# First mixer: S5 input products in two PSUM pools, LRU tiles emitted in five steps

## The chip, the cores and the metric

One core of a Trainium2 chip runs the whole program. The metric is the device time in microseconds (us), the median of the runs. Five engines appear below: PE (TensorE matmuls; PEld is its weight loads), DVE (VectorE), ACT (ScalarE), POOL (GpSimd) and SP (SyncE, which issues the DMAs). Each works through its own queue in order and waits at an instruction until what that needs is done.

## The reference, cut to what matters

The program is a trunk of two layers on 1040 tokens of width 1024 (16 learned meta tokens are put in front of 1024). Each layer is a token mixer and an MLP with squared ReLU, each added to the residual. The change lies in the first mixer, which projects the normed input to 12 blocks of 128 features (four blocks x for the LRU, four blocks g for its gate, four blocks u for S5), and then:

```
x  = causal conv of width 4 over tokens (x)                    # per feature
r  = sigmoid(block_diag(x, w_a) + b_a);  i = sigmoid(block_diag(x, w_x) + b_x)
a  = exp(-8 * r * softplus(-lam));       m = sqrt(1 - a*a)
h[t] = a[t] * h[t-1] + m[t] * i[t] * x[t]                      # scan over tokens
y_lru = h * gelu(g)
# S5: 32 groups of 16 channels, 64 complex states each
s[t] = A * s[t-1] + B u[t];  y = real(C s) + d * u
y_s5 = gelu(y) * sigmoid(block_diag(gelu(y), w_glu) + b_glu)
out  = concat(y_lru, y_s5) @ w_out
```

## The kernel before

Features lie on the 128 partitions and tokens along the free dimension, cut in three stretches of 400, 384 and 256 (`TT`). A projection product is done as three float32r matmuls of split operands (`mm3`: high by high, high by low, low by high), so a *unit* (`unit`), one block of 128 output features for one stretch of tokens, is 8 x 3 = 24 matmuls into one PSUM bank, followed by a conversion on DVE (L969 for u, L978 for x, L984 and L986 for g). PSUM has eight banks here, in two pools of four: `mm` (`self.mm()`, used by units, the LRU gates, the S5 products and the S5 gate) and `sm` (`self.sm()`, used by the norm sums and the S5 tables).

`ev_units` gives 36 units in a fixed order, numbered 0 to 35 in the texts: u0 and u1 interleaved (0 to 5), u2 (6 to 8), u3 (9 to 11), x0 (12 to 14), x1 (15 to 17), g0 (18 to 20), x2 (21 to 23), x3 (24 to 26), g1 (27 to 29), and g2 and g3 mixed (30 to 35). The loop at the end of `mixer0` calls `events()` ahead of unit n and then emits the unit. Other work is hung onto these events by `at(n, (key, generator))`; the events of one n run in the order of their keys:

- S5 is computed in eight batches of four groups. `s5_tables` builds the matrices of a batch (L793 to L795 on DVE, transposes L806 and products L807 on PE, L813 on DVE, then L824 on PE and L826 on ACT). `s5_batch` loads the input of the batch, makes the input products (L848, L849) in two rounds, each with two PSUM tiles `va` and `vb`, multiplies them with rotations (L852, L853, L854), scans (L856), rotates back (L858 on POOL, L859) and makes the output products (L866 to L868). `s5_tile` takes two batches together: gelu (L884), gate matmul (L886), tanh (L887), and the product L888, which writes block 4 + t of the residual tile `h`.
- After the third unit of an x block, whose conversions are followed by the convolution (`lru_conv`: L900 on ACT, three L902 on DVE), `lru_tile` is run for that block: at n = 15, 18, 24 and 28 for blocks 0, 1, 2 and 3.

`lru_tile` has 48 instructions: six gate matmuls (L917) with sigmoids (L918), tanh, exp and a product (L920 to L922), a Newton step for the square root (L925 to L929), and per stretch a square root (L932), two products (L933 on DVE; L934 on POOL, for the last stretch on DVE) and the scan (L935). Its gate tiles `l_tr` and `l_ti` have one buffer each, so the sigmoids of one block wait until the scans of the block before are done. Its temporaries `th` and `q` are blocks 6 and 7 of `h`, which `s5_tile` writes for t = 2 and 3.

The order on each engine is not the program's: the framework's scheduler takes, for an engine that is free in its own model of time, the ready instruction of the highest priority. The priority is the place in the program, and `high_priority(offset=-100)` moves the instructions in it 100 places back (L60 to L63 set these offsets for the decorated functions; `lru_tile` has -100 in the first mixer). So a late place decides only among ready instructions. PSUM and SBUF tiles of a pool are given out in the order in which the scheduler comes to them.

Of the kernel before, what the change touches and what calls it, by code (L numbers as in the profile page):

```python
# [13 lines left out]
AF = mybir.ActivationFunctionType  # L14
ALU = mybir.AluOpType
# [7 lines left out]
TT = [(0, 400), (400, 384), (784, 256)]  # L23
# [55 lines left out]
class Trunk:  # L79
# [749 lines left out]
    def s5_batch(self, pool, b):  # L829

        nc, s5 = self.nc, self.s5
        v = nc.vector
        ud, yd = (q[b // 2][(b % 2) * 64:(b % 2) * 64 + 64] for q in (self.ud, self.yd))
        gs = slice(NG * b, NG * b + NG)
        ug = pool.tile([P, NG, 130], F32, name="s5ug", bufs=2)
        for g in range(NG):
            nc.sync.dma_start(ug[:, g], ud[16 * g:16 * g + 16].rearrange("c j n -> j c n"))
        yield
        M2, F, G, Z = self.tab[b]
        C, Sn = Z[:, 0], Z[:, 1]  # L840
        w = pool.tile([P, NG, 131], F32, name="s5w")
        w2 = pool.tile([P, NG, 131], F32, name="s5w2")
        v.memset(w[:, :, 0:1], 0.0)
        for g0 in range(0, NG, 2):
            n = 2
            va, vb = self.mm(), self.mm()
            for g in range(n):
                nc.tensor.matmul(va[:, g * 130:g * 130 + 130], lhsT=M2[:, g0 + g, 0:P], rhs=ug[:, g0 + g], start=True, stop=True)  # L848
                nc.tensor.matmul(vb[:, g * 130:g * 130 + 130], lhsT=M2[:, g0 + g, 64:192], rhs=ug[:, g0 + g], start=True, stop=True)  # L849
            v3 = lambda q: q[:, :n * 130].rearrange("p (g c) -> p g c", g=n)  # L850
            sl = (slice(None), slice(g0, g0 + n), slice(1, 131))
            v.tensor_tensor(out=w[sl], in0=v3(va), in1=C[sl], op=ALU.mult)  # L852
            v.tensor_tensor(out=w2[sl], in0=v3(vb), in1=Sn[sl], op=ALU.mult)  # L853
            v.tensor_tensor(out=w[sl], in0=w[sl], in1=w2[sl], op=ALU.add)  # L854
        for g in range(NG):
            v.tensor_tensor_scan(out=w[:, g, 1:], data0=s5["rho"][:, NG * b + g:NG * b + g + 1].broadcast_to([P, 130]), data1=w[:, g, 1:],  # L856
                                 initial=0.0, op0=ALU.mult, op1=ALU.add)
        nc.gpsimd.tensor_tensor(out=w2[:, :, 0:130], in0=w[:, :, 0:130], in1=Sn[:, :, 0:130], op=ALU.mult)  # L858
        v.tensor_tensor(out=w, in0=w, in1=C, op=ALU.mult)  # L859
        yield  # L860
        yg = pool.tile([P, NG, 130], F32, name="s5yg")
        m2 = lambda q: q.rearrange("p j i -> p (j i)")
        M1 = self.tab.pop(b)[4]
        for g in range(NG):
            pt = self.mm()
            nc.tensor.matmul(pt[:, :130], lhsT=m2(M1[:, g]), rhs=ug[:, g], start=True, stop=False)  # L866
            nc.tensor.matmul(pt[:, :130], lhsT=m2(F[:, g]), rhs=w[:, g, 0:130], start=False, stop=False)
            nc.tensor.matmul(pt[:, :130], lhsT=m2(G[:, g]), rhs=w2[:, g, 0:130], start=False, stop=True)  # L868
            nc.scalar.copy(yg[:, g], pt[:, :130])
        for g in range(NG):  # L870
            nc.sync.dma_start(yd[16 * g:16 * g + 16].rearrange("c j n -> j c n"), yg[:, g])
# [29 lines left out]
        for k in (2, 1, 0):  # L901
            nc.vector.scalar_tensor_tensor(out=xc, in0=xr[:, o + k:o + k + w], scalar=cw(k), in1=xc, op0=ALU.mult, op1=ALU.add)  # L902

    @shifted
    def lru_tile(self, pool, t):

        nc = self.nc
        v = nc.vector
        tr, ti = (pool.tile([P, NTOK], F32, name=n) for n in ("l_tr", "l_ti"))
        c = self.m0c  # L910
        m4, m8 = c["m4sp"][:, t:t + 1], c["m8sp"][:, t:t + 1]
        xc, th, q = ([self.h[i][:, k] for i in range(3)] for k in (t, 6, 7))
        trs, tis = ([d[:, o:o + w] for o, w in TT] for d in (tr, ti))
        for i, (o, w) in enumerate(TT):
            for j, d in enumerate((trs, tis)):
                pt = self.mm()
                nc.tensor.matmul(pt[:, :w], lhsT=c["gates"][:, j, t], rhs=xc[i], start=True, stop=True)  # L917
                nc.scalar.activation(out=d[i], in_=pt[:, :w], func=AF.Sigmoid, bias=self.col(("ba", "bx")[j], t))  # L918
        for i in range(3):
            nc.scalar.activation(out=th[i], in_=trs[i], func=AF.Tanh, scale=m4)  # L920
            nc.scalar.activation(out=q[i], in_=trs[i], func=AF.Exp, scale=m8)
            (nc.gpsimd if i < 2 else v).tensor_tensor(out=tis[i], in0=tis[i], in1=xc[i], op=ALU.mult)  # L922
        for i in range(3):
            m = trs[i]
            nc.scalar.activation(out=q[i], in_=q[i], func=AF.Copy, scale=0.5, bias=0.5)  # L925
            v.scalar_tensor_tensor(out=m, in0=th[i], scalar=-1.0, in1=q[i], op0=ALU.add, op1=ALU.mult)
            v.scalar_tensor_tensor(out=q[i], in0=m, scalar=2.0, in1=q[i], op0=ALU.add, op1=ALU.mult)
            v.tensor_tensor(out=m, in0=th[i], in1=q[i], op=ALU.mult)
            nc.scalar.activation(out=m, in_=m, func=AF.Identity, scale=2.0, bias=1.0)  # L929
        ini = 0.0  # L930
        for i, (o, w) in enumerate(TT):
            nc.scalar.activation(out=th[i], in_=th[i], func=AF.Sqrt, scale=-4.0)  # L932
            v.tensor_tensor(out=q[i], in0=q[i], in1=th[i], op=ALU.mult)  # L933
            (nc.gpsimd if i < 2 else v).tensor_tensor(out=tis[i], in0=tis[i], in1=q[i], op=ALU.mult)  # L934
            v.tensor_tensor_scan(out=xc[i], data0=trs[i], data1=tis[i], initial=ini, op0=ALU.mult, op1=ALU.add)  # L935
            ini = xc[i][:, w - 1:w]

    def unit(self, wt, i, tls, evac, more=0):

# [94 lines left out]
    def mixer0(self):  # L1034
        nc, tc, A = self.nc, self.tc, self.A
        with tc.tile_pool(name="m0c", reuse_waits="tile", bufs=1) as cpool, tc.tile_pool(name="m0", reuse_waits="tile", bufs=1) as m0:
# [46 lines left out]
            def at(n, g):  # L1083
                ev.setdefault(n, []).append(g)


            for b, s in enumerate((10, 13, 16, 19, 22, 25, 27, 30)):
# [7 lines left out]
                if b % 2:  # L1095
                    g = self.s5_tile(m0, b // 2)
                    for j in range(3, 7):
                        at(s + j, (1, g))
            n = 6
            lru = {}  # L1100
            gates, split = 0, 0

            def events():
                for _, g in sorted(ev.pop(n, []), key=lambda e: e[0]):
                    next(g, None)
                if n in lru:

                    assert self.s5_out < 2
                    self.lru_tile(m0, lru[n])

            while True:
                events()
                if gates == 1 and split == 0:
                    self.wo0 = self.load_w(A["ev_out"][0])
                while split < min(gates, self.s5_done):
                    self.split_y(split)
                    split += 1
                u = next(units, None)
                n += 1
                if u is None:  # L1120
                    if split == 3:
                        break
                    continue
                q, i = u
                if q[0] == "x":
                    self.lru_conv(int(q[1]), i, self.xr[int(q[1])])
                    if i == 2:
                        lru[n + (q == "x3")] = int(q[1])
                gates += q == "g3"
# [582 lines left out]
```

## Time and profile before

| | us |
|---|---|
| median of 3 runs (lowest, highest) | 2751.69 (2750.94, 2755.02) |
| the profiled execution, its own time | 2751.07 |
| its span in the trace | 2749.3 |
| busy: PE, DVE, ACT, POOL | 2664.6, 1963.5, 1076.9, 1034.7 |

Busy times are those of the whole span; an engine that waits at an instruction is idle. The granted clock of PE is given as a share of full speed (1.00 is 2.4 GHz, 0.50 is 1.2 GHz), averaged over the stretch asked for. Times in the trace count from the start of the span. The first mixer ends, and the output projection begins, at about 289 us.

### The profile page before, as it was taken

Reading aid. Unit: us, or ns where it says so; the run is one execution under the profiler, and the core shown is the slowest. Engines: PE = TensorE matmul, PEld = TensorE weight load, DVE = VectorE, ACT = ScalarE, POOL = GpSimd, SP = SyncE. Lnnn points to the kernel's source line nnn. Section 1 sums busy time; section 2 is a strip of 40 time slices with the busy share of each in tenths; the row PEclk is TensorE's granted clock in tenths of the full one; section 3 lists DMA queues with packets and bytes.
Section 4 is the critical chain, followed back from the end, with each engine's and each line's share of the span. In section 5 each row is a group of like instructions: output and inputs, shape, how many; then the busy total and the mean of one; then the engine's idle time right before and its main releaser. Section 6 shows DMA issues by size and latency. Waiting matters only on the chain.

```text
span 2749.3 us, 44507 instructions
## 1 busy us (share of the span) xinstructions
PE 2664.6 (97%) x17121; PEld 2551.6 (93%) x17121; DVE 1963.5 (71%) x3877; ACT 1076.9 (39%) x2207; POOL 1034.7 (38%) x842
## 2 busy tenths in 40 slices
PE   7998999999999999999999999999989999999998
PEld 7887999999999999899999999998988999999998
DVE  9887465666666686876767767677786666666685
ACT  5565344233233233453434434344454333333334
POOL 2122115454444532142233322333444554554542
PEclk9989999999999999999999999999999999999999
DMA  4422411111111110121211212123311111111111
GB/s 165 112 76 57 148 47 47 47 54 43 51 51 47 51 39 29 44 94 59 69 62 60 76 59 69 62 60 97 109 55 64 54 51 50 54 50 50 47 43 62
DMA packets 117909, 176.35 MB, mean 64 GB/s; under 512 B 13376, under 2 KB 47936, under 8 KB 117568
## 3 DMA queue, kind: packets, MB, share of 16 engines
q1 hardware_dynamic: 117408, 173.34, 20.3%
q8 instruction: 135, 2.21, 0.3%
q14 instruction: 78, 0.64, 0.1%
q10 hardware_dynamic: 288, 0.15, 0.0%
HBM read 158.34 MB, written 8.72 MB: 61 GB/s over the span
## 4 chain that ended last, share of the span: by engine, by line
PE 51%; DVE 6%; ACT 1%; DMA 1%; POOL 1%; issue 0%; DVEq 0%; ACTq 0%; POOLq 0%; SPq 0%
PE mm L182 12%; PE mm L183 12%; PE mm L184 12%; PE pd L182 3%; PE pd L184 3%; PE pd L183 3%; DVE xbc L1272 1%; PE mm L1392 1%; PE sm L1396 1%; PE mm L1389 1%; PE sm L1358 1%; DMA csb<-csd 1%; PE sm L253 1%; PE sm L270 0%; PE sm L1372 0%
## 5 line engine op out<-in xcount | busy, mean ns | idle before, releaser
L182 PE MATMUL mm<-hi,whi 128*128 128x384 f32 (+4 forms) x3120 | 1019.0, 327 | 16.1 <-ACT whi L176 8.6
L183 PE MATMUL mm<-lo,whi 128*128 128x384 f32 (+4 forms) x3120 | 1007.5, 323 | 0.9 <-DVE lo L300 0.5
L184 PE MATMUL mm<-hi,wlo 128*128 128x384 f32 (+4 forms) x3120 | 1004.2, 322 | 2.3 <-POOL wlo L177 2.3
L182 PEld LDWEIGHTS mm<-hi,whi 128*128 128x128 f32 x3120 | 591.0, 189 | 26.0 <-ACT whi L176 9.4
L183 PEld LDWEIGHTS mm<-lo,whi 128*128 128x128 f32 x3120 | 590.9, 189 | 7.2 <-DVE lo L300 0.8
L184 PEld LDWEIGHTS mm<-hi,wlo 128*128 128x128 f32 x3120 | 592.5, 190 | 3.3 <-POOL wlo L177 3.0
L182 PE MATMUL pd<-pc 128*128 128x260 f32 (+1 forms) x1176 | 377.0, 321 | 6.3 <-DVE s L375 2.2
L184 PE MATMUL pd<-pc 128*128 128x260 f32 (+1 forms) x1176 | 374.7, 319 | 0.0
L183 PE MATMUL pd<-pc 128*128 128x260 f32 (+1 forms) x1176 | 373.6, 318 | 0.0
L492 DVE TENSOR_TENSOR h<-h,pd 128x520 f32<-128x520 f32 (+1 forms) x336 | 291.8, 870 | 59.6 <-PE pd L184 45.2
L375 DVE SCALAR_TENSOR_TENSOR s<-mm,rb 128x384 f32<-128x384 f32 (+2 forms) x192 | 98.6, 514 | 265.1 <-PE mm L184 252.2
L389 POOL TENSOR_TENSOR pc<-ca,pc 128x512 fp32r<-128x512 f32 x112 | 169.8, 1516 | 244.8 <-ACT pc L388 164.1
L389 POOL TENSOR_TENSOR pc<-draw,pc 128x512 fp32r<-128x512 f32 x84 | 125.1, 1489 | 338.2 <-ACT pc L388 338.2
L182 PEld LDWEIGHTS pd<-pc 128*128 128x128 f32 x1176 | 221.5, 188 | 22.1 <-DVE acc L492 4.5
L184 PEld LDWEIGHTS pd<-pc 128*128 128x128 f32 x1176 | 221.6, 188 | 15.9
L183 PEld LDWEIGHTS pd<-pc 128*128 128x128 f32 x1176 | 221.6, 188 | 12.5
L176 ACT CAST whi<-wraw 128x512 fp32r<-128x512 f32 x286 | 167.6, 616 | 164.1 <-PE mm L183 150.2
L376 ACT ACTIVATE sq<-s 128x384 f32<-128x384 f32 (+2 forms) x192 | 94.1, 490 | 347.1 <-DVE s L375 347.0
L492 DVE TENSOR_TENSOR acc<-acc,pd 128x520 f32<-128x520 f32 (+1 forms) x234 | 190.3, 861 | 4.2 <-PE pd L184 4.1
L177 DVE TENSOR_TENSOR wlo<-wraw,whi 128x512 fp32r<-128x512 f32 x224 | 167.0, 764 | 18.1 <-ACT whi L176 9.4
L1378 POOL TENSOR_TENSOR csb<-csb,sc 128x512 f32<-128x512 f32 x64 | 89.7, 1402 | 210.3 <-DVE sc L1374 199.1
L388 ACT CAST pc<-cb 128x520 fp32r<-128x520 f32 (+1 forms) x112 | 70.0, 625 | 247.2 <-PE pd L184 130.4
(390 smaller groups left out, 4531.6 us busy)
## 6 DMA issues: line engine op xcount, KB each, us to landing
wraw<-in_mlp_up SPq DMA_DIRECT2D x128, 256.0 KB
wraw<-in_ssd_in SPq DMA_DIRECT2D x120, 256.0 KB
draw<-in_mlp_down SPq DMA_DIRECT2D x112, 256.0 KB
csb<-csd SPq DMA_DIRECT2D x64, 256.0 KB
ecb<-ecd SPq DMA_DIRECT2D x128, 64.0 KB
wraw<-in_ssd_out SPq DMA_DIRECT2D x32, 256.0 KB
wraw<-in_ev_in SPq DMA_DIRECT2D x24, 256.0 KB
wraw<-in_ev_out SPq DMA_DIRECT2D x18, 256.0 KB
```

Source lines behind the costliest of these rows:

```text
L176: nc.scalar.copy(h, raw)
L177: e.tensor_tensor(out=l, in0=raw, in1=h.bitcast(F32), op=ALU.subtract)
L182: nc.tensor.matmul(pt, lhsT=whi, rhs=xhi, start=first, stop=False)
L183: nc.tensor.matmul(pt, lhsT=whi, rhs=xlo, start=False, stop=False)
L184: nc.tensor.matmul(pt, lhsT=wlo, rhs=xhi, start=False, stop=last)
L253: nc.tensor.matmul(st[:l, 508 + i:509 + i], lhsT=a[:, o:o + l], rhs=self.ones, start=j == 0, stop=j == len(accs) - 1)
L375: nc.vector.scalar_tensor_tensor(out=r, in0=pt[:, :w], scalar=0.0, in1=rbs[i], op0=ALU.max, op1=ALU.mult)
L376: nc.scalar.activation(out=dst[:, o - t0:o - t0 + w].bitcast(F32), in_=r, func=AF.Square)
L388: nc.scalar.copy(hi, x)
L389: e.tensor_tensor(out=lo, in0=x, in1=hi.bitcast(F32), op=ALU.subtract)
L492: v.tensor_tensor(out=d, in0=d, in1=src, op=ALU.add)
L1378: nc.gpsimd.tensor_tensor(out=csb, in0=csb, in1=sc.unsqueeze(1).broadcast_to([P, 4, P]), op=ALU.mult)
```

## The change

Of the two tiles of an S5 round, `vb` is taken from the `sm` pool and no longer from `mm`. `lru_tile` loses its decorator and becomes a generator of five steps, each emitted 50 places back: gates and sigmoids; tanh, exp, products and the Newton step of stretch 0; the Newton steps of stretches 1 and 2 and all square roots; the products and scan of stretch 0; those of stretches 1 and 2. For blocks 0 to 2 the first two steps are emitted at the event where the whole tile was, and the others at the events of the next three units, with key 4; for block 3 all five are emitted at once. The arithmetic is the same. The order within a tile differs in that the square roots of all stretches come before the first product L933.

```diff
--- before.py
+++ after.py
@@ -843,7 +843,7 @@
         v.memset(w[:, :, 0:1], 0.0)
         for g0 in range(0, NG, 2):
             n = 2
-            va, vb = self.mm(), self.mm()
+            va, vb = self.mm(), self.sm()
             for g in range(n):
                 nc.tensor.matmul(va[:, g * 130:g * 130 + 130], lhsT=M2[:, g0 + g, 0:P], rhs=ug[:, g0 + g], start=True, stop=True)
                 nc.tensor.matmul(vb[:, g * 130:g * 130 + 130], lhsT=M2[:, g0 + g, 64:192], rhs=ug[:, g0 + g], start=True, stop=True)
@@ -901,7 +901,6 @@
         for k in (2, 1, 0):
             nc.vector.scalar_tensor_tensor(out=xc, in0=xr[:, o + k:o + k + w], scalar=cw(k), in1=xc, op0=ALU.mult, op1=ALU.add)
 
-    @shifted
     def lru_tile(self, pool, t):
 
         nc = self.nc
@@ -911,29 +910,50 @@
         m4, m8 = c["m4sp"][:, t:t + 1], c["m8sp"][:, t:t + 1]
         xc, th, q = ([self.h[i][:, k] for i in range(3)] for k in (t, 6, 7))
         trs, tis = ([d[:, o:o + w] for o, w in TT] for d in (tr, ti))
-        for i, (o, w) in enumerate(TT):
-            for j, d in enumerate((trs, tis)):
-                pt = self.mm()
-                nc.tensor.matmul(pt[:, :w], lhsT=c["gates"][:, j, t], rhs=xc[i], start=True, stop=True)
-                nc.scalar.activation(out=d[i], in_=pt[:, :w], func=AF.Sigmoid, bias=self.col(("ba", "bx")[j], t))
-        for i in range(3):
-            nc.scalar.activation(out=th[i], in_=trs[i], func=AF.Tanh, scale=m4)
-            nc.scalar.activation(out=q[i], in_=trs[i], func=AF.Exp, scale=m8)
-            (nc.gpsimd if i < 2 else v).tensor_tensor(out=tis[i], in0=tis[i], in1=xc[i], op=ALU.mult)
-        for i in range(3):
+        later = lambda: self.tc.high_priority(offset=-50)
+
+        def newton(i):
             m = trs[i]
-            nc.scalar.activation(out=q[i], in_=q[i], func=AF.Copy, scale=0.5, bias=0.5)
             v.scalar_tensor_tensor(out=m, in0=th[i], scalar=-1.0, in1=q[i], op0=ALU.add, op1=ALU.mult)
             v.scalar_tensor_tensor(out=q[i], in0=m, scalar=2.0, in1=q[i], op0=ALU.add, op1=ALU.mult)
             v.tensor_tensor(out=m, in0=th[i], in1=q[i], op=ALU.mult)
             nc.scalar.activation(out=m, in_=m, func=AF.Identity, scale=2.0, bias=1.0)
-        ini = 0.0
-        for i, (o, w) in enumerate(TT):
-            nc.scalar.activation(out=th[i], in_=th[i], func=AF.Sqrt, scale=-4.0)
+
+        def scan(i):
+            o, w = TT[i]
             v.tensor_tensor(out=q[i], in0=q[i], in1=th[i], op=ALU.mult)
             (nc.gpsimd if i < 2 else v).tensor_tensor(out=tis[i], in0=tis[i], in1=q[i], op=ALU.mult)
-            v.tensor_tensor_scan(out=xc[i], data0=trs[i], data1=tis[i], initial=ini, op0=ALU.mult, op1=ALU.add)
-            ini = xc[i][:, w - 1:w]
+            v.tensor_tensor_scan(out=xc[i], data0=trs[i], data1=tis[i], initial=xc[i - 1][:, TT[i - 1][1] - 1:] if i else 0.0,
+                                 op0=ALU.mult, op1=ALU.add)
+
+        with later():
+            for i, (o, w) in enumerate(TT):
+                for j, d in enumerate((trs, tis)):
+                    pt = self.mm()
+                    nc.tensor.matmul(pt[:, :w], lhsT=c["gates"][:, j, t], rhs=xc[i], start=True, stop=True)
+                    nc.scalar.activation(out=d[i], in_=pt[:, :w], func=AF.Sigmoid, bias=self.col(("ba", "bx")[j], t))
+        yield
+        with later():
+            for i in range(3):
+                nc.scalar.activation(out=th[i], in_=trs[i], func=AF.Tanh, scale=m4)
+                nc.scalar.activation(out=q[i], in_=trs[i], func=AF.Exp, scale=m8)
+                (nc.gpsimd if i < 2 else v).tensor_tensor(out=tis[i], in0=tis[i], in1=xc[i], op=ALU.mult)
+            for i in range(3):
+                nc.scalar.activation(out=q[i], in_=q[i], func=AF.Copy, scale=0.5, bias=0.5)
+            newton(0)
+        yield
+        with later():
+            newton(1)
+            newton(2)
+            for i in range(3):
+                nc.scalar.activation(out=th[i], in_=th[i], func=AF.Sqrt, scale=-4.0)
+        yield
+        with later():
+            scan(0)
+        yield
+        with later():
+            scan(1)
+            scan(2)
 
     def unit(self, wt, i, tls, evac, more=0):
 
@@ -1106,7 +1126,12 @@
                 if n in lru:
 
                     assert self.s5_out < 2
-                    self.lru_tile(m0, lru[n])
+                    g = self.lru_tile(m0, lru[n])
+                    for _ in range(5 if lru[n] == 3 else 2):
+                        next(g, None)
+                    if lru[n] < 3:
+                        for d in range(1, 4):
+                            at(n + d, (4, g))
 
             while True:
                 events()
```

## Rows read from the trace of the kernel before

**Rows 1.** Stretches: busy us (count) of PE, PEld, DVE, ACT, POOL; clock, DMA.

```profile
100.00:285.00 185.00, 163.50 (x1004) 150.93 (x1003) 150.29 (x316) 117.04 (x222) 42.06 (x32) 0.93 0.29 75
...
285.00:2740.00 2455.00, 2416.30 (x15623) 2319.86 (x15621) 1716.81 (x3209) 917.03 (x1894) 970.29 (x775) 1.00 0.19 60
```

**Rows 2.** Timeline, PE: start us, us, what; in brackets idle before, releaser.

```profile
138.62 2.90 PE L917 MATMUL mm<-h,gates 128*128 128x384 f32 x4 [2.57 <-DVE h L902]
...
142.95 2.00 PE L824 MATMUL sm<-s5kk,ident 128*128 128x64 f32 x16 [1.43 <-DVE s5kk L813]
...
145.82 0.48 PE L806 MATMUL sm<-ident,s5E 128*128 128x128 f32 x1 [0.87 <-DVE s5E L795]
...
172.81 2.79 PE L824 MATMUL sm<-s5kk,ident 128*128 128x64 f32 x12 [1.65 <-DVE s5kk L813]
...
227.81 0.70 PE L182 MATMUL mm<-hi,whi 128*128 128x400 f32 x1 [5.66 <-DVE s5w L852]
...
263.38 1.22 PE L886 MATMUL mm<-s,gluw 128*128 128x256 f32 x2 [5.30 <-ACT s L884]
```

**Rows 3.** Stretches around the gaps, and two of DVE.

```profile
136.00:153.00 17.00, 12.13 (x49) 9.84 (x49) 15.75 (x23) 11.94 (x21) 7.09 (x7) 0.70 0.27 72
171.00:180.00 9.00, 7.35 (x30) 7.24 (x29) 8.56 (x20) 2.95 (x9) 1.05 (x1) 0.62 0.43 115
222.00:231.00 9.00, 3.34 (x12) 3.19 (x12) 9.00 (x16) 2.41 (x3) 4.01 (x4) 0.81 0.50 154
258.00:269.00 11.00, 5.70 (x20) 5.44 (x20) 11.00 (x18) 4.26 (x8) 3.32 (x2) 0.69 0.15 48
181.90:238.00 56.10, 49.40 (x316) 44.90 (x314) 51.92 (x112) 31.93 (x63) 13.30 (x9) 0.97 0.29 73
238.00:250.00 12.00, 12.00 (x87) 11.61 (x87) 1.53 (x4) 11.38 (x22) 1.99 (x2) 1.00 0.16 39
```

**Rows 4.** Timeline, DVE, 136 to 143 us.

```profile
136.20 1.76 DVE L935 TENSOR_TENSOR_SCAN h<-l_tr,l_ti 128x400 f32<-128x400 f32 x1 [0.92 <-POOL l_ti L934]
...
137.89 0.59 DVE L902 SCALAR_TENSOR_TENSOR h<-ux,cols,h 128x384 f32<-128x384 f32 x1
...
142.82 0.74 DVE L935 TENSOR_TENSOR_SCAN h<-l_tr,h,l_ti 128x256 f32<-128x256 f32 x1
```

**Rows 5.** Timeline, DVE, 219 to 228 us.

```profile
219.93 0.99 DVE L935 TENSOR_TENSOR_SCAN h<-l_tr,l_ti 128x400 f32<-128x400 f32 x1 [0.91 <-POOL l_ti L934]
...
222.90 2.01 DVE L935 TENSOR_TENSOR_SCAN h<-l_tr,h,l_ti 128x384 f32<-128x384 f32 x1
...
227.36 0.40 DVE L852 TENSOR_TENSOR s5w<-mm,s5Z 128x260 f32<-128x260 f32 x1
```

**Rows 6.** Timeline, DVE, 171 to 173 us.

```profile
171.66 0.87 DVE L933 TENSOR_TENSOR h<-h 128x384 f32<-128x384 f32 x2
172.45 0.22 DVE L813 TENSOR_TENSOR s5kk<-sm,s5dm 128x64 f32<-128x64 f32 x1
```

**Rows 7.** Timeline, PE and ACT, from unit 17 to unit 18.

```profile
129.17 0.28 PE L184 MATMUL mm<-hi,wlo 128*128 128x256 f32 x1
...
134.47 1.59 PE L917 MATMUL mm<-h,gates 128*128 128x400 f32 x4
...
145.59 1.28 ACT L918 ACT_TABLE_LOAD   x1
...
146.88 0.59 ACT L918 ACTIVATE l_tr<-mm,cols 128x400 f32<-128x400 f32 x1
...
149.47 0.90 PE L182 MATMUL mm<-hi,whi 128*128 128x400 f32 x1
```

**Rows 8.** Timeline, DVE and ACT, 261 to 263 us.

```profile
261.06 1.03 DVE L933 TENSOR_TENSOR h<-h 128x400 f32<-128x400 f32 x2
...
262.01 2.35 DVE L888 SCALAR_TENSOR_TENSOR h<-s5y,s 128x400 f32<-128x400 f32 x2
...
262.91 0.42 ACT L884 ACTIVATE s<-s5y 128x256 f32<-128x256 f32 x1 [0.33 <-DVE h L888]
```

## The prediction

> **What bounds the kernel now.** I first read the table by stage, then TensorE's (PE's) list of gaps, then the granted clock around each gap, then VectorE (DVE) and ScalarE (ACT) just ahead of each gap. From 285 us to 2740 us PE is busy 2416.3 of 2455 us at a granted clock of 1.00; from 100 to 285 us, where the change lies, it is busy 163.5 of 185 us at 0.93 [rows 1]. So the rest of the kernel takes over any microsecond won or lost in the first mixer, and the mixer holds what there is to win. DVE is busy 150.3 of the same 185 us [rows 1]: a second engine nearly as full, whose work the change does not shorten.
>
> PE's idle time there is four places, which I call A to D [rows 2]. A, 136 to 146 us: 2.57 us for the convolution L902, 1.43 for L813, 0.87 for L795. B, 172.8: 1.65 for L813. C, 227.8: 5.66 for L852, which frees the PSUM bank the next unit wants. D, 263.4: 5.30 for the gelu L884. Together 17.5 us. Each is followed by a stretch at the lower of the two clock levels (1.2 instead of 2.4 GHz); what that costs is (1 - granted clock) x length of the window around it [rows 3]: A 0.30 x 17 = 5.1, B 0.38 x 9 = 3.4, C 0.19 x 9 = 1.7, D 0.31 x 11 = 3.4 us. So A is worth 10.0 us, B 5.1, C 7.4, D 8.7: 31.2 us in all. That is the ceiling of the change, and nothing reaches it unless DVE also keeps up.
>
> **The change part by part.** No arithmetic is removed or added: the same 48 LRU instructions of a tile on the same engines and shapes, the same S5 products. What moves is (1) which PSUM banks the second half of the S5 products takes, and (2) the place of the LRU instructions in the order. No DMA is issued by the moved steps, so the queues of SP and POOL are passed by nothing; POOL's multiplies L922 and L934 move with their step.
>
> *Banks, at C.* The S5 products of a batch take four `mm` tiles, all of that pool; so unit 27 waits for DVE's first product L852, which comes at 227.36, behind the scans of LRU tile 2 (from 219.93) [rows 5]. With two of the four in the `sm` pool the next unit finds an `mm` bank, and PE could start at 227.81 - 5.66 = 222.15 [rows 2]. Upper end: all 7.4 us. The `sm` pool has then five tiles a batch in four banks (two transposes, two products, the M1 matmul); the batches are two or three units apart, and a unit is 8.7 us here (units 18 to 27 start at 149.47 and 227.81, nine units in 78.3 us [rows 2, 7]), so each is read long before its bank comes round; I price that at nothing, and at one wait like B's, 1.65 us, if DVE is late there. Lower end for C: from 181.9 to 238.0 DVE is busy 51.9 of 56.1 us [rows 3], so a PE that starts 5.7 us earlier may stand at the next DVE result instead; then 0. I take 5, near the upper end, because the LRU scans, which delay that next result, are moved back too.
>
> *Scans later, at A, B and C.* Before, a whole tile carries one priority, 100 instructions late. After, each step is 50 late from its own place, and the places are one unit apart. A tile's gates, tanh, exp and first Newton step therefore come about 50 instructions (one unit) earlier than the later ones; the scans come one to one and a half units later. At A the first scan ran 136.20 to 137.96 and held up the convolution L902, for which PE's gates of tile 1 waited; the last scan began at 142.82, among what PE's next wait, for L813, had to see done [rows 2, 4]. At B the two multiplies L933 (0.87 us) are just ahead of L813 at 172.45 [rows 6]. With the scans one unit on, the convolutions and L813 run ahead of them. B: L813 itself takes 0.22 us and cannot go [rows 6], so at most 1.4 of the 1.65 us and the clock stretch, 4.8 in all: 0 to 4.8, I take 3, since the clock stretch goes only if the gap does. A: 0 to 10.0, and below nothing (see the first rival). I take 3, near the lower end, because of its second half: the gates of tile 1 went to PE at 134.47, but their first sigmoid ran at 146.88, since `l_tr` and `l_ti` have one buffer and tile 0's last scan ended at 143.56; unit 18 could start only at 149.47, when banks came free [rows 4, 7]. That wait the change does not remove.
>
> *Added wait.* With the last scan of tile 0 and the gates of tile 1 emitted at the same event (n = 18), the sigmoids of tile 1 wait on a DVE instruction that is now of low priority. Queued behind them on ACT are the casts, the S5 copies and the gelus; on PE the gate matmuls that find no bank, and every unit behind them.
>
> *Tile 3, at D.* All five steps stay in one place but 50 instead of 100 late. D's chain: from 238 to 250 us DVE has 1.5 us of work in 12, waiting for ACT [rows 3]; then Newton, the multiplies L933 end at 262.0, the S5 result L888 follows at 262.01 because it overwrites what L933 reads, and the gelu L884 at 262.91 waits for L888's scratch [rows 8]. 50 instructions earlier is about the instructions of one unit with its conversions: at least its 24 matmuls, 3.3 us at the pace of 238 to 250 us (87 matmuls in 12.0 us [rows 3]), at most the 8.7 us of a whole unit. Against D's 5.30 us of gap and 3.4 of clock that is 0 to 8.7. I take 3, near the lower pace, because PE, freed at C, also arrives earlier at D, and then the chain has to be earlier by as much.
>
> *Activation tables.* Each change of function set costs ACT 1.28 us, and the sigmoid starts right behind the load, 145.59 + 1.28 = 146.87 against 146.88 [rows 7]. Five steps over four units mix LRU functions with more gelus. Four to eight more loads are 5 to 10 us on an engine that is busy 117.0 of 185 us [rows 1]: hidden, but for the part in a chain that PE awaits. Zero to 5 us; I take 1.3, one load in D's chain. The Trainium skill (ScalarE: Activation LUTs, What ACT_TABLE_LOAD costs) gives about 2.66 us for a switch, the load and a drain of about 1.38 us; by that the term would be an estimated 2.7 us. The trace shows no such drain.
>
> *New small waits.* PE has many hand-overs of 0.2 to 0.9 us with DVE here, and a PE that is ahead meets more of them: 0 to 5 us, I take 2.7.
>
> Sum: 5 (C) + 3 (B) + 3 (A) + 3 (D) - 1.3 - 2.7 = 10 us. The profiled execution took 2751.07 us (span 2749.3 and 1.8 around it), 0.6 below the median of 2751.69; 2751.07 - 10 = 2741.1, and by the median 2741.7. I say 2741.5.
>
> **The rivals.** *Slower: the gates hold the banks.* Place: unit 18 (tiles 0 and 1) and again units 27 to 28 (tiles 2 and 3). Low-priority gates take all `mm` banks while their sigmoids wait for the previous tile's last scan. That scan is one unit later than before, 3.3 to 8.7 us at each place (the two paces of a unit above; I take 5), and it lengthens D's chain by as much. Twice 5 and one more low-clock stretch of 3.4 are 13.4 us lost; with 7.4 won at C and no more, the time is 2751 + 6 = 2757. It decides once the last scan of tile 0 ends more than 14 us after unit 17, the distance of before (129.45 to 143.56 [rows 4, 7]). For it: the same jam is in the trace, 134.47 to 149.47 [rows 7]. Against: DVE's scans ran slowly there (the 384-column scan at 222.90 took 2.01 us, beside POOL's work, where the 400-column one took 0.99) [rows 5], and a scan elsewhere may be twice as fast; and the convolutions are now out of the way of the gates.
>
> *No change: DVE is the bound.* PE is free at C but then waits at the next gates or transposes, since DVE's 51.9 of 56.1 us stay [rows 3]; B goes, A and D stay: 2751 - 3 = 2748. For it: DVE's share. Against: DVE's 12 us with 1.5 us of work at 238 to 250 [rows 3], into which work can slide. That the change does not do what it says belongs here: a ready instruction of low priority still goes when its engine has nothing else, so the order on DVE may hardly differ.
>
> *Most of the ceiling.* If all four gaps close and their clock stretches with them, 31.2 less 4 to 7 of new waits: about 2726.
>
> **How the numbers follow.** About 0.2% (5.5 us) is what a measurement here can tell from no change. The forecast's own band, 5.5 to 17 us faster, has 0.50; most of the ceiling 0.12; no change 0.20; slower 0.18. Faster is thus 0.62. The range for 8 in 10: low 2727 (most of the ceiling), high 2757 (the slower rival); the forecast's own is 2734 to 2746.
>
> **What would show it.** Right: unit 27 starts within a microsecond of the products L849 ahead of it; in PE's waits the 5.7 us for L852 and the 2.6 us for L902 are gone; the granted clock from 100 us to the end of the mixer is above 0.95; from then on PE is full, about 10 us earlier than before. A step is wrong if the gap is there under another name: at C a wait for L902 or L795; at A gate matmuls more than 12 us ahead of their sigmoid. The prediction fails if the mixer ends at the same time with the gaps elsewhere, or if the time differs after 300 us more than before it.

## The result: 16 us slower, where 10 us faster was forecast

The kernel after takes 2767.73 us (median of 6 runs, 2765.15 to 2770.9); in the same runs the kernel before takes 2751.64 (6 runs, 2748.52 to 2755.02). The ratio is 1.0058, 95% interval [1.0048, 1.0069]. The forecast was 2741.5, its range ended at 2757.

The profiled execution of after took 2765.15 us, its span is 2763.4, 14.1 longer than before. The output projection begins at 302.75 us, and at 289.12 before: 13.6 of the 14.1 us are lost in the first mixer. Its stretches, in the columns of [rows 1]:

```profile
100.00:285.00 185.00, 147.10 (x878) 134.07 (x877) 140.29 (x300) 135.95 (x223) 34.94 (x29) 0.89 0.26 68
285.00:2740.00 2455.00, 2418.54 (x15610) 2322.42 (x15609) 1712.03 (x3191) 918.77 (x1897) 967.91 (x772) 1.00 0.19 59
```

In the mixer PE's busy time and clock have fallen (163.50 to 147.10 us, 0.93 to 0.89), DVE's busy time too (in the same 185 us, of a mixer that now ends 13.6 us later), and only ACT's has risen, 117.04 to 135.95 us.

PE's timeline at the places of [rows 2] (start us, us, what; in brackets the idle time before and what ended it). Unit 27 now follows its products at once: C is closed. At A the gates still wait 2.65 us for the convolution L902. New gaps stand ahead of each of the three lines that name ACT:

```profile
130.78 1.70 PE L886 MATMUL mm<-s,gluw 128*128 128x400 f32 x2 [4.73 <-ACT s L884]
...
149.20 1.10 PE L933 MATMUL mm<-h,gates 128*128 128x256 f32 x4 [2.65 <-DVE h L902]
...
174.63 0.70 PE L182 MATMUL mm<-hi,whi 128*128 128x400 f32 x1 [5.89 <-ACT s5yg L869]
...
224.54 0.39 PE L849 MATMUL sm<-s5ug,s5M 128*128 128x130 f32 x2
...
226.47 0.43 PE L182 MATMUL mm<-hi,whi 128*128 128x400 f32 x1
...
267.12 1.24 PE L849 MATMUL sm<-s5ug,s5M 128*128 128x130 f32 x4 [7.49 <-ACT s5M L810]
```

PE's waits from 60 to 320 us by what ended them (total us, times, longest). Before, DVE ended nearly all of them and ACT one, D's 5.30 us; now ACT leads the list:

```profile
PE sm L849 <- ACT s5M L810: 9.2, 3, 7.5
PE mm L886 <- ACT s L884: 6.9, 3, 4.7
PE mm L182 <- ACT s5yg L869: 5.9, 1, 5.9
PE mm L933 <- DVE s L1004: 5.0, 1, 5.0
```

Why ACT is late is plain when its instructions are grouped. ACT's table loads, 60 to 320 us, kernel before, then after (busy us, mean ns | idle before). L934 is the sigmoid and L939 the exp; before they were L918 and L921:

```profile
L921 ACT ACT_TABLE_LOAD x6 | 7.7, 1283 | 0.0
...
L918 ACT ACT_TABLE_LOAD x4 | 5.1, 1283 | 0.1
```

```profile
L934 ACT ACT_TABLE_LOAD x16 | 20.5, 1283 | 0.3
L939 ACT ACT_TABLE_LOAD x12 | 15.4, 1283 | 0.1
```

With the lines of other functions it is 24 loads before and 45 after. The 21 more are 26.9 us; ACT's busy time from 60 to 320 us rises by 25.3 (140.50 to 165.77). The timelines show where they come from. Tile 3 before: sigmoids up to 240.82, one load, and then tanh and exp in turns without any, up to the load of a gelu (L985) at 244.69:

```profile
240.34 0.48 ACT L918 ACTIVATE l_ti<-mm,cols 128x256 f32<-128x256 f32 x1
240.71 0.62 ACT L920 ACTIVATE h<-l_tr,m4sp 128x400 f32<-128x400 f32 x1
241.33 1.28 ACT L921 ACT_TABLE_LOAD   x1
242.63 0.63 ACT L921 ACTIVATE h<-l_tr,m8sp 128x400 f32<-128x400 f32 x1
243.16 0.60 ACT L920 ACTIVATE h<-l_tr,m4sp 128x384 f32<-128x384 f32 x1
```

Tile 3 after: the first two stretches each run sigmoid, sigmoid, tanh, load, exp, load, and then come the sigmoids of the next stretch:

```profile
238.71 1.28 ACT L934 ACT_TABLE_LOAD   x1
240.00 0.59 ACT L934 ACTIVATE l_tr<-mm,cols 128x400 f32<-128x400 f32 x1
240.50 0.59 ACT L934 ACTIVATE l_ti<-mm,cols 128x400 f32<-128x400 f32 x1
240.97 0.63 ACT L938 ACTIVATE h<-l_tr,m4sp 128x400 f32<-128x400 f32 x1
241.60 1.28 ACT L939 ACT_TABLE_LOAD   x1
242.90 0.63 ACT L939 ACTIVATE h<-l_tr,m8sp 128x400 f32<-128x400 f32 x1
243.54 1.28 ACT L934 ACT_TABLE_LOAD   x1
244.84 0.58 ACT L934 ACTIVATE l_tr<-mm,cols 128x384 f32<-128x384 f32 x1
```

The tanh needs no load behind a sigmoid (240.97) and none behind an exp (before, 243.16), so of these three only the step from sigmoid to exp and back costs one. The trace agrees in this with the Trainium skill (ScalarE: Activation LUTs, Table sets: the hidden batching unit), which lists tanh in the sigmoid's set and in the exp's.

Twenty microseconds on, the same queue holds up PE:

```profile
259.82 1.28 ACT L949 ACT_TABLE_LOAD   x1
261.11 0.52 ACT L949 ACTIVATE h<-h 128x384 f32<-128x384 f32 x1
...
261.96 1.28 ACT L934 ACT_TABLE_LOAD   x1
263.25 0.47 ACT L934 ACTIVATE l_ti<-mm,cols 128x256 f32<-128x256 f32 x1
...
264.61 1.28 ACT L949 ACT_TABLE_LOAD   x1
265.91 0.42 ACT L949 ACTIVATE h<-h 128x256 f32<-128x256 f32 x1
...
266.69 0.38 ACT L810 COPY s5M<-sm 128x256 f32<-128x256 f32 x1
```

The copy L810 at 266.69 is what PE waits for, for 7.49 us, at 267.12. Among what stands ahead of it in ACT's queue, while PE stands still, are three loads, two square roots and the last sigmoid of tile 3, 13 us behind the fifth (250.05).

### The profile page after: what moved, and what is told of

Same layout as the page of the kernel before. It is cut to its first block, busy times and chain, and to the rows that moved or that the text cites. A ratio compares the mean times of both kernels' runs of the same rounds, so it can differ in the third digit from the quotient of the medians.

```text
span 2763.4 us, 44524 instructions
## 1 busy us (share of the span) xinstructions
PE 2663.8 (96%) x17121; PEld 2550.4 (92%) x17121; DVE 1960.4 (71%) x3877; ACT 1105.3 (40%) x2228; POOL 1032.9 (37%) x842
## 4 chain that ended last, share of the span: by engine, by line
PE 50%; DVE 6%; ACT 1%; DMA 1%; POOL 1%; issue 1%; SPq 0%; DVEq 0%; ACTq 0%; POOLq 0%
PE mm L182 12%; PE mm L183 12%; PE mm L184 12%; PE pd L182 3%; PE pd L184 3%; PE pd L183 3%; DVE xbc L1297 1%; PE mm L1417 1%; PE sm L1421 1%; PE mm L1414 1%; PE sm L1383 1%; DMA csb<-csd 1%; PE sm L253 1%; PE sm L270 1%; PE sm L1397 0%
```

## The experiments

Theory L: the loads are the loss. As I read the framework, a `high_priority` block takes the program's place less its offset and gives the place back at its end. Two blocks emitted with nothing between them would therefore begin at the same place, and their instructions rank beside each other, not one behind the other. So tanh and exp of stretch 0 (step 1) rank no later than the sigmoids of stretch 1 (step 0). No run shows the places themselves; ACT's order in the trace above is what they would give. The rival, theory B, is the change of banks; rivals O and O2 (the order, or the spread over four units) came later. The expectations of the two Exp runs, of the added loads and of the five steps in one block count the loads of the whole first mixer, two at its start with them; the others, and all counts below, go from 60 to 320 us and have two fewer. Differences below are between medians of runs on the same chip; kernels that ran on different chips are each taken against the kernel before on their own. The edits shown are cut to what matters.

**The two parts alone.** The banks alone, and the five steps alone:

```diff
-            va, vb = self.mm(), self.mm()
+            va, vb = self.mm(), self.sm()          # banks alone: only this line
```

> The bank change alone; lru_tile is that of before. Theory L (activation table loads: the two steps emitted at one event are placed from the same place, so that sigmoids and exps alternate; 21 more loads of 1.28 us in the first mixer): this program has 28 loads in the mixer against 24 before and 45 after, so the time stays near before, 2744 to 2756 us, and the wait for L852 (5.7 us) is gone. Rival B (the bank change: the products in the other pool are put ahead of what they read, and PE stands at L849 for the M2 copies of ACT): 2760 to 2770 us, with waits of L849 for L810 of 5 us or more.

> The five steps alone; both tiles of an S5 round come from the pool mm as before. L: 46 loads in the mixer, so as slow as the changed kernel or slower, 2763 to 2775 us, ACT busy about 20 us more between 100 and 300 us. B: no slower than before, at most 2756 us.

Banks alone: 2740.6 us against 2753.49, ratio 0.9954 [0.994, 0.9967], 12.9 us faster, the largest gain of all kernels here. Five steps alone: 2776.63, 1.0081 [1.0066, 1.0097], 23.1 us slower, 1.6 us above the range of theory L, with 46 loads. Theory B falls. The banks gain more than theory L expected of them, which gave 2744 us at best; as far as it is known, why is told below.

**One block in place of two, and two in place of one.** The whole change with steps 0 and 1 in one block, and the kernel before with its one block cut behind the sigmoids:

```diff
                     nc.scalar.activation(out=d[i], in_=pt[:, :w], func=AF.Sigmoid, ...)
-        yield
-        with later():
             for i in range(3):
                 nc.scalar.activation(out=th[i], in_=trs[i], func=AF.Tanh, scale=m4)
```

> The changed kernel with its first two steps in one block of one priority (gates, sigmoids, tanh, exp, first Newton step), four steps over the same units; banks as changed. L: the six sigmoids of a tile stand together again, 25 loads; the loss is gone and what the change was to win may show: 2738 to 2752 us. B: the loss stays, 2760 to 2770 us.

```diff
                     nc.scalar.activation(out=d[i], in_=pt[:, :w], func=AF.Sigmoid, ...)
+        with self.tc.high_priority(offset=-100):      # the lines above stand in such a block of their own
             for i in range(3):
                 nc.scalar.activation(out=th[i], in_=trs[i], func=AF.Tanh, scale=m4)
```

> The kernel before with nothing changed but that the gates and sigmoids of lru_tile stand in one block of priority -100 and the rest in a second block of -100, at the same event. Nothing is spread over units and no bank is changed. L: 44 loads, 2762 to 2775 us. B: as before, 2748 to 2756 us.

The change with one block: 2748.12 us, 0.9981 [0.9972, 0.999], 5.4 us faster than before, where the change with two is 16.1 slower. In its trace there are 25 loads, 20 fewer than after, and the six sigmoids of a tile stand together, but for a tanh in tile 0 that makes no load (ACT, tile 1):

```profile
140.80 1.28 ACT L934 ACT_TABLE_LOAD   x1 [4.18 <-DVE h L926]
142.10 0.59 ACT L934 ACTIVATE l_tr<-mm,cols 128x400 f32<-128x400 f32 x1
...
144.35 0.51 ACT L934 ACTIVATE l_ti<-mm,cols 128x256 f32<-128x256 f32 x1
144.71 0.66 ACT L936 ACTIVATE h<-l_tr,m4sp 128x400 f32<-128x400 f32 x1
145.37 1.28 ACT L937 ACT_TABLE_LOAD   x1
```

The kernel before with its block cut in two, and nothing else: 2773.29, 1.0072 [1.0059, 1.0084], 19.8 us slower, with 44 loads. The cut itself makes the loads and the loss; banks and spread aren't needed for it.

**The loads by themselves.** The cut or the order could still cost in another way. So loads were added to the kernel before, without the cut:

```diff
                 nc.scalar.activation(out=d[i], in_=pt[:, :w], func=AF.Sigmoid, ...)
+                if 1 <= 2 * i + j <= 3:
+                    nc.scalar.activation(out=th[i][:, :1], in_=trs[i][:, :1], func=AF.Exp)
```

> The kernel before, with three one-column Exps per LRU tile between the sigmoids of its gates (into a column that the tanh overwrites); nothing else moves. In the compiled program the first mixer has 53 table loads where the kernel before has 26, at 1.283 us each. Theory L (the loads themselves cost, because they stand in the chain gate, sigmoid, exp that TensorE comes to wait for): 27 loads are 35 us of ACT, of which half to nine tenths show, 2768 to 2784 us, ratio 1.006 to 1.011, and ACT is named as the releaser of TensorE's longest waits. Rival O (it is the order of the work that two blocks from one place make, and the loads are hidden beside TensorE): 2750 to 2757 us, ratio under 1.0015.

2775.2 us against 2751.64, 1.0087 [1.0074, 1.01]: 23.6 us slower for 27 more loads (51 in the trace), in the middle of what L expected, far from O. The small Exps themselves are only 2.4 us. Loads and Exps of its trace, then its longest wait of PE:

```profile
L918 ACT ACT_TABLE_LOAD x15 | 19.2, 1283 | 2.8 <-DVE h L937 2.6
L920 ACT ACT_TABLE_LOAD x11 | 14.1, 1283 | 0.2
...
L920 ACT ACTIVATE h<-l_tr 128x1 f32<-128x1 f32 x12 | 2.4, 202 | 0.1
```

```profile
PE mm L886 <- ACT s L884: 12.1, 1, 12.1
```

That is gap D, 5.30 us before, 12.1 with the loads. Per load the kernel loses 23.6 / 27 = 0.87 us, about two thirds of its 1.283. The loads didn't come quite alone, though the expectation says so: other instructions took other places with them. In tile 3 the sixth sigmoid starts at 264.42 us, 7.2 us behind the fifth, where before it followed at once (239.91 and 240.34). So this run shows the loads together with a new order, and the next pair has to tell the order apart.

**The order without the loads.** Exp in the place of Sigmoid puts gates, tanh and exp into one table, in the kernel after and, as its reference, in the kernel before:

```diff
-                 ... func=AF.Sigmoid, bias=self.col(("ba", "bx")[j], t))
+                 ... func=AF.Exp, bias=self.col(("ba", "bx")[j], t))
```

> The kernel after, with Exp for Sigmoid in the gates (values are others, sizes and order are the same): gates, tanh and exp now use one table, so the two blocks from one place no longer make loads; 23 in the first mixer where the kernel after has 47. Read against the same edit of the kernel before. Theory L: the loss goes, and with the banks' gain the time is 3 to 13 us below that of the kernel before with Exp, 2732 to 2745 us. Rival O (the order itself costs): 10 to 18 us above the kernel before with Exp, as the kernel after is above the kernel before.

> The kernel before with Exp for Sigmoid in the gates, the reference for the other Exp run; 22 loads in the first mixer where the kernel before has 26. Theory L: four loads fewer, 2745 to 2752 us. Rival O: the same as before within 2 us, 2750 to 2755.

After: 2740.38 us; before: 2752.16 (both against 2751.64; ratios 0.996 [0.9948, 0.9972] and 0.9998 [0.999, 1.0007]). With 21 and 20 loads, the whole change with its two blocks is 11.8 us faster. Inside all four tiles the order of gates, tanh and exp is nearly that of the kernel after, two gates, a tanh, an exp and again. Rival O expected it 10 to 18 slower, and falls. Only tile 3's last gate is not as late as after: it starts 1.6 us behind the fifth (234.63 and 233.07) and not 13, so what that lateness would cost without loads isn't shown. The reference lies where O expected it, just above L's range: six loads fewer at the gates and exps (L918, L921) and two more at other lines buy nothing that can be told (interval 2.8 us faster to 1.9 slower).

**The spread without banks or alternation.** The five steps alone, the first two in one block (26 loads):

> The five steps of the change without its banks, with the first two steps in one block, so that sigmoids and exps don't alternate; 28 loads in the first mixer, against 48 with the five steps alone (2776.6 us). Theory L: the loss of the five steps goes, 2748 to 2760 us, ratio 0.998 to 1.003. Rival O2 (spreading a tile over four units costs by itself, since its scans come later): most of the loss stays, 2768 to 2777 us, ratio 1.006 to 1.009.

2754.98 us, 1.0011 [1.0002, 1.0021], 3.3 us slower, where with two blocks it was 23.1. Most of the loss goes, and O2 falls. But the spread gains nothing either, though it closes gap C (see below).

**What is left, 50 or 100 places.** Banks alone is 7.5 us faster than the one-block change (2740.6 and 2748.12, on the same chip). Two kernels ask whether the places or the spread do it:

```diff
-         "lru_tile": -100          # banks alone, 50 places late in place of 100
+         "lru_tile": -50
-        later = lambda: self.tc.high_priority(offset=-50)     # one-block change, 100 in place of 50
+        later = lambda: self.tc.high_priority(offset=-100)
```

> The banks alone, with the whole LRU tile 50 places late in place of 100. Asks where the 7.5 us between the banks alone (2740.6 us) and the one-block version of the whole change (2748.1 us) go. Theory M (the places: 50 late and not 100, the tile's work stands ahead of projection work that TensorE awaits sooner): 2745 to 2752 us. Theory S (the spread over four units: the scans come late, and with them what follows): 2738 to 2743 us, as with the banks alone.

> The one-block version of the whole change (banks, gates and exps in one block, four steps over four units), with each step 100 places late in place of 50. Theory M: 2738 to 2743 us, as with the banks alone. Theory S: 2745 to 2752 us, as with each step 50 late.

2745.17 us, 0.9984 [0.9975, 0.9993], and 2746.51, 0.9982 [0.9973, 0.999], against 2751.25. Neither theory foresaw that both would lose. Of the banks' gain of 12.9 us they leave 6.1 and 4.7, where both differences together leave 5.4: each takes back 7 or 8 us, and both together no more. In the first, PE's longest wait is now for the S5 copies L869 (5.5 us), which it doesn't have with 100 places. Why both lose is open.

## Where the time went, stretch by stretch

Length of the stretches between starts of units in us, with the table loads in them from 60 us on, from the traces (the output projection is the end of the mixer):

| | before | after | one block | banks alone | before with loads |
|---|---|---|---|---|---|
| start to unit 14 | 102.23 (0) | 94.99 (0) | 95.59 (0) | 96.86 (0) | 101.41 (0) |
| unit 14 to 18 | 47.24 (9) | 56.54 (16) | 48.11 (7) | 51.29 (6) | 55.99 (18) |
| unit 18 to 24 | 50.42 (5) | 54.47 (10) | 52.75 (8) | 47.55 (10) | 53.85 (13) |
| unit 24 to 27 | 27.92 (3) | 20.47 (5) | 22.68 (2) | 25.74 (3) | 28.54 (5) |
| unit 27 to output projection | 61.31 (7) | 76.28 (14) | 66.07 (8) | 59.21 (9) | 71.63 (15) |
| output projection starts | 289.12 | 302.75 | 285.20 | 280.65 | 311.42 |

After against one block loses 8.4 us from unit 14 to 18 and 10.2 us from unit 27 on, where it has 9 and 6 loads more. Before with loads loses in the same two stretches against before: 8.8 and 10.3 us, with 9 and 8 loads more (from unit 18 to 24, 8 more cost only 3.4). Two kernels with different orders lose nearly the same in the same places, and the loads are what they share.

With the banks alone the table holds 8.5 us of gain; the two profiled executions differ by 8.8 (2742.23 and 2751.07), the medians by 12.9. Not every stretch gains: from unit 14 to 18 it loses 4.1 us.

The first line is a gain that I did not see. From 70 to 90 us the kernel before runs PE at 0.68 and 0.80 of its clock, after small waits of 0.2 to 0.7 us around the S5 products:

```profile
70.00:80.00 10.00, 9.03 (x55) 8.79 (x54) 9.87 (x24) 2.63 (x6) 0.47 (x1) 0.68 0.77 182
80.00:90.00 10.00, 10.00 (x61) 10.00 (x61) 5.20 (x23) 1.39 (x4) 1.20 (x1) 0.80 0.11 33
```

With the banks alone PE doesn't stop from 70 to 80 us, and the clock stays up:

```profile
70.00:80.00 10.00, 10.00 (x77) 10.00 (x76) 8.56 (x19) 1.77 (x4) 0.00 (x0) 1.00 0.73 175
80.00:90.00 10.00, 9.62 (x72) 9.32 (x71) 9.75 (x31) 2.91 (x8) 1.39 (x2) 1.00 0.38 120
```

From 60 to 70 us it is the other way round, 1.00 before and 0.85 with the banks. So, in this pair, the clock gives (0.32 + 0.20 - 0.15) x 10 = 3.7 us, and PE's busy time from 60 to 100 us rises from 38.22 to 39.62, 1.4 us less of waiting: 5.1 of the 5.4 us by which unit 14 comes sooner. The other traces bear it out: in all six kernels with the new banks the clock from 70 to 90 us is 1.00 and unit 14 starts at 94.9 to 96.9 us, in all six with the old ones it is 0.68 to 0.92 and unit 14 starts at 100.8 to 103.1. The 0.85 from 60 to 70 us doesn't belong to the banks: one of the six with the old ones has 0.84 there, and the other five with the new ones 1.00.

## Why the prediction was wrong

The step that failed is *Activation tables*: "Four to eight more loads are 5 to 10 us ... hidden, but for the part in a chain that PE awaits ... I take 1.3". There were 21 more, 26.9 us of ACT, and they cost some 20 us: 21.5 between the change with two blocks and with one (20 loads), 19.8 between the five steps alone with two and with one (20 loads), 19.8 by the cut alone (20 loads), 23.6 by loads added without the cut (27). The number came wrong from the step before it, "each step is 50 late from its own place, and the places are one unit apart". That holds for steps 2 to 4 of tiles 0 to 2. Steps 0 and 1 are emitted at one event and, as I now read it, share a place; I had read the two blocks as a sequence. The second half of the error was to price the loads as cover, 117.0 busy of 185 us: the sigmoids stand between the gates' banks and the next unit, and what PE needs from ACT (L810, L869, L884) stands behind them in ACT's queue, so a load there isn't covered by ACT's idle time elsewhere. My price also came from one place, D's chain; against the one-block change the kernel after loses in two, 8.4 us from unit 14 to 18 and 10.2 from unit 27 on.

The other terms, with the loads set aside:

- **C, 5 us forecast for the banks.** The wait for L852 is gone, as forecast, and unit 24 to 27 is 7.45 us shorter after (27.92 to 20.47), my upper end. But unit 24 starts 6.1 us later there; with the banks alone the stretch is only 2.2 us shorter. The banks' 12.9 us come from elsewhere too: they give 5.4 us ahead of unit 14 (102.23 to 96.86), a stretch I left out because I looked for gaps from 100 us on. With them most of D goes as well. PE's timeline with the banks alone: at B L824 follows without a gap, at C unit 27 follows its products, and at D 1.84 us are left of 5.30:

```profile
171.75 1.90 PE L824 MATMUL sm<-s5kk,ident 128*128 128x64 f32 x16
...
220.61 1.18 PE L848 MATMUL mm<-s5ug,s5M 128*128 128x130 f32 x4
221.44 0.68 PE L182 MATMUL mm<-hi,whi 128*128 128x400 f32 x1
...
255.06 0.70 PE L886 MATMUL mm<-s,gluw 128*128 128x256 f32 x2 [1.84 <-ACT s L884]
```

- **B, A and D, 3 us each for the later scans.** Not earned by the scans: the five steps in one block without the banks are 3.3 us slower, not 9 faster. They do close gaps, C among them, with the old banks: unit 27 follows L824 at 223.90 us, the stretch from unit 24 is 24.03 us in place of 27.92, and D is 1.76.

```profile
222.15 1.90 PE L824 MATMUL sm<-s5kk,ident 128*128 128x64 f32 x16
223.90 0.45 PE L182 MATMUL mm<-hi,whi 128*128 128x400 f32 x1
```

But from unit 27 on that kernel takes 66.23 us in place of 61.31, with new waits of PE that DVE ends, of 2.40 us for L1002, 1.75 for L795 and 3.24 for L859. That is what my rival "DVE is the bound" says; no run tests it. With the banks alone, the tile whole and 100 late, B's gap is gone from its place (a wait of 1.71 us for L813 stands at 216.03 instead) and D's falls to 1.84. So the late scans aren't needed for D, and A's wait for L902 stays with the banks alone (2.99 us) as after (2.65). How the banks help D wasn't tried apart. My reading of A was also off: L813 ran ahead of the last scan (142.82), which so wasn't among what PE's wait for L813 had to see done. DVE, kernel before:

```profile
142.69 0.21 DVE L813 TENSOR_TENSOR s5kk<-sm,s5dm 128x64 f32<-128x64 f32 x1
```

- **The sum.** Banks -12.9 and spread +3.3 would be -9.6; the one-block change measures -5.4; the 4.2 us between them are no more than the intervals of the three ratios allow, so an interplay isn't shown. The forecast of 10 us was near what the change does without its loads (11.8 with Exp for Sigmoid), but by other terms than mine: that is luck.
- **`sm` at nothing.** It didn't quite hold. With the banks alone L849, which now writes an `sm` tile, waits three times for ACT's L810, which it didn't before; L810 reads an `sm` tile and writes what L849 reads, and the trace doesn't tell which of the two it waits for. PE's waits, banks alone:

```profile
PE sm L849 <- ACT s5M L810: 2.1, 3, 1.5
```

- **New small waits, 2.7 forecast.** With the banks alone these 2.1 us and 3.0 us more for L902 (5.6 in place of 2.6) make some 5, the upper end of my range.
- **The slower rival, gates that hold the banks.** The time went to its side, but not by its mechanism. It was to decide if tile 0's last scan ended over 14 us after unit 17. PE's last matmul of unit 17 and DVE's last scan of tile 0, in the kernel after, are 6 us apart:

```profile
135.58 0.28 PE L184 MATMUL mm<-hi,wlo 128*128 128x256 f32 x1
...
141.17 0.73 DVE L926 TENSOR_TENSOR_SCAN h<-l_tr,h,l_ti 128x256 f32<-128x256 f32 x1
```

Units did wait for a bank that a sigmoid (L934) still had to read, but only 2.5 us in all.

- **What would show it.** Unit 27 behind L849 and the end of the L852 wait came true; the L902 wait stayed; the clock was 0.89 and not over 0.95. Of the sign that I named for failure, "the mixer ends at the same time with the gaps elsewhere", the waits show the gaps elsewhere, under ACT's name; the mixer ends 13.6 us later. No rival of mine had ACT as the new bound.

## What to carry to other kernels

Before a chain is cut into steps, look at which step's instructions will rank beside which, and count the function sets in ACT's queue in that order: a sigmoid that alternates with an exp pays 1.28 us each time. Keep the sigmoids of one tile in one block. Engine totals don't price this: ACT was busy 63% of the 185 us before and 73% after, and still became what PE waited for, because loads stood in its queue ahead of copies that PE needs. And a change of two parts is better run as two: here one line is the whole gain (2740.6 us), and the rest loses it.

## What the runs showed of the hardware

- A table load, 1.283 us on ACT each time, has different prices by its place. With 27 added the kernel lost 23.6 us; in the traces 9 of them cost 8.8 us from unit 14 to 18, and 8 only 3.4 from unit 18 to 24.
- Waits of 0.2 to 0.7 us between 68 and 74 us go with a PE clock of 0.68 and 0.80 of full speed from 70 to 90 us, so that PE, shown busy for 19.03 of these 20 us, ran part of them at the lower level (1.2 GHz). With the banks alone, without the waits, the clock there is 1.00. A list of PE's idle times doesn't show that loss; the granted clock does.
